# Fixed state places, a decay taken a step ahead and a pinned order in the state-space stage of a hybrid trunk layer

## The chip, the cores and the metric

The kernel runs on one core of a Trainium2 chip. The metric is the device time of one execution in microseconds, lower is better; the median of several runs is given. A core has five engines that run their own instruction queues in order and wait for each other through semaphores: TensorE (PE in the profile; its weight loads are listed apart as PEld), VectorE (DVE), ScalarE (ACT), GpSimd (POOL) and SyncE (SP), which here only issues DMA transfers. SBUF is the on-chip memory that all engines read; PSUM is the small memory of eight banks that TensorE writes its products to, and from which VectorE and ScalarE read.

## The reference

One layer of width 1024 on a sequence of 1024, everything in float32. A wide projection of the normalised input feeds two branches. The first (y_a) is a gated spatial mixer. The second (y_b) is a chunked state-space scan with 32 heads of 64 in 8 groups, a state of 128 and chunks of 128. Both are projected, gated, added and projected out. The part that matters here is the scan:

```python
decay = segsum_exp(adt)
cb = jnp.einsum('bclgn,bcsgn->bcgls', cc, bc)
y_diag = jnp.einsum('bcgls,bcgrls,bcsgrp->bclgrp', cb, decay, xd)
decay_to_end = jnp.exp(a_cs[..., -1:] - a_cs)
chunk_states = jnp.einsum('bcsgn,bcgrs,bcsgrp->bcgrpn', bc, decay_to_end, xd)
chunk_decay = jnp.exp(a_cs[..., -1])

def step(state, inp):
    cs, cd = inp
    return state * cd[..., None, None] + cs, state
...
y_off = jnp.einsum('bclgn,bcgrpn,bcgrl->bclgrp', cc, prev_states, jnp.exp(a_cs))
return (y_diag + y_off)
```

Then y_b gets the skip term (d_skip times x), is multiplied with silu(z) and RMS-normalised within its group.

## The kernel before

The kernel is one long program. Large products are made from three passes of a high and a low part of each operand ("hi" by ScalarE's copy, "lo" by VectorE's subtraction). It runs in stages: input and modulation, the wide projection (line 536), the state-space stage interleaved with the projection of y_a (this case), the projection of y_b (line 1548) and the output projection (line 1741).

**Order.** The instructions are written in Python and a planner decides the order on each engine from an estimated timeline. Two things bind it. `pin` (line 78) makes an instruction keep its program order among all pinned instructions of its engine: every TensorE instruction is pinned, and so are the loads on SyncE's queue. `tc.high_priority()` lets instructions go ahead of others that are ready. What is not pinned goes where the planner puts it. On the chip each queue is then strictly in order.

**The stage.** `order` (line 1202) lists 32 steps: two groups run interleaved, and each group has four steps of two chunks (256 positions). For step n the loop at line 1419 runs `front` of n, some units of the y_a projection (`draw`), `back` of n, `prep` of n + 2, the loads (`fetch`) of n + 5 and the decays of n + 3. A `draw` unit is two matmuls of `proj_a` (line 1355). Tasks given to `later(delay, ...)` run after so many slots; each `front`, `back` and `prep` is one slot.

- `fetch` loads the cumulative log decays (tile dcy, broadcast to all partitions) and the slab sl with six parts: C, B, two parts of x, two of silu(z). Five sets of these tiles rotate.
- `decay` (line 1058): ScalarE's exponential into ea (line 1063), GpSimd's triangular mask on dcy (line 1066), eight exponentials on dcy by ScalarE (line 1071).
- `prep` (line 1073): TensorE makes C·B and the transpose of B into bank pc and the transposes of x into bank px. VectorE makes xd and xe from px (line 1087) and multiplies dcy with C·B (line 1091); ScalarE copies the transposed B to tile bn (line 1093).
- `front` (line 1096): 16 matmuls give the within-chunk part in bank yi, then two or four give the chunk states in bank sp. For both chunks GpSimd multiplies the group's state with the chunk's decay into a new tile (line 1119) and VectorE adds sp to it (line 1121); the first state of a group is a copy (line 1117). The state tiles come from a rotation of four places over both groups (`st_r`).
- `back` (line 1125): eight matmuls (four in a group's first step) of the two states before the chunks with C give bank yn. `evacuate` (line 1138): VectorE adds the skip term to yi (y, line 1147) and multiplies yn with ea (ym, line 1151); GpSimd adds both (line 1152) and multiplies with silu(z) into yz (line 1153).
- `post` (line 1155): every second step of a group yz is stored; `squares` (line 1170) squares it in place on ScalarE (line 1172) and adds the halves on GpSimd (line 1173); `post2` sums over the group with TensorE and VectorE's ssq (line 1182).
- `proj_a` (line 1355): eight blocks of 8 x 3 units; at k = 1 of a block `wa_block` (line 1272) splits the weights of the next block: ScalarE's copy wah (line 1276) and VectorE's subtraction wal (line 1277), two of each. A block ends with the gate products tha on VectorE (line 1378).

Of the kernel before, what the change touches and what calls it, by code (L numbers as in the profile page):

```python
# [8 lines left out]
F32 = mybir.dt.float32  # L9
# [7 lines left out]
P = 128  # L17
# [18 lines left out]
def hybrid_kernel(  # L36
# [46 lines left out]
    def tp(dst, src, idn):  # L83
        pin(PE.transpose(dst, src, idn))  # L84
# [948 lines left out]
    NSET = 5  # L1033
    nstep, nst = [0], [0]

    class Group:
# [36 lines left out]
        def prep(self, s):  # L1073
            g, nm = self.g, f"{self.g}_{s}"
            sl, dcy, ea = self.pre[s]
            px, pc = bank(f"px{nm}"), bank(f"pc{nm}")
            for i in range(2):
                tsl = slice(i * P, (i + 1) * P)
                mm(pc[:, i * P : (i + 1) * P], sl[:, 1, tsl], sl[:, 0, tsl])
                tp(pc[:, 256 + i * P : 256 + (i + 1) * P], sl[:, 1, tsl], ident)  # L1080
                tp(px[:, i * 256 : i * 256 + P], sl[:, 2, tsl], ident)
                tp(px[:, i * 256 + P : i * 256 + 256], sl[:, 3, tsl], ident)
            x4 = px.rearrange("p (i h w) -> p i h w", i=2, h=HPG)
            xs = []
            for v, f in (("xd", dthq), ("xe", dde)):
                t = p2x.tile([P, 512], F32, name=f"{v}{nm}", tag=v, bufs=3)
                V.tensor_tensor(t.rearrange("p (i h w) -> p i h w", i=2, h=HPG), x4,
                                fac(f, g, s).unsqueeze(3).to_broadcast([P, 2, HPG, HD]), op=ALU.mult)
                xs.append(t)
            d3 = dcy.rearrange("p h i l -> p h (i l)")  # L1090
            V.tensor_tensor(d3, d3, pc[:, 0:256].unsqueeze(1).to_broadcast([P, HPG, 256]), op=ALU.mult)  # L1091
            bn = p2x.tile([P, 256], F32, name=f"bn{nm}", tag="bn", bufs=3)
            A.copy(bn, pc[:, 256:512])
            self.pre[s] = (sl, dcy, bn, xs[0], xs[1], ea)

        def front(self, s):
# [10 lines left out]
            sp = bank(f"sp{nm}")  # L1107
            self.y[s] = yi
            self.sts = [self.st]
            for i in range(2 if s < NCH // 2 - 1 else 1):  # L1110
                mm(sp[:, i * 256 : (i + 1) * 256], bn[:, i * P : (i + 1) * P], xe[:, i * 256 : (i + 1) * 256])
            for i in range(2 if s < NCH // 2 - 1 else 1):
                pool, tag, b = st_r[nst[0] % 4 if nst[0] % 4 < 3 else 2]
                nst[0] += 1
                s2 = pool.tile([P, 512 if pool is hp else 256], F32, name=f"st{nm}_{i}", tag=tag, bufs=b)[:, 0:256]
                if self.st is None:
                    V.tensor_copy(s2, sp[:, 0:256])
                else:
                    G.tensor_mul(v3(s2), v3(self.st),  # L1119
                                 fac(cd, g, s)[:, i].unsqueeze(2).to_broadcast([P, HPG, HD]))  # L1120
                    V.tensor_add(s2, s2, sp[:, i * 256 : (i + 1) * 256])  # L1121
                self.st = s2
                self.sts.append(s2)

        def back(self, s):
# [12 lines left out]
        def evacuate(self, s, yi, yn):  # L1138

# [4 lines left out]
            yz = self.yz[s // 2][:, :, (s % 2) * 256 : (s % 2 + 1) * 256]  # L1144
            y1 = turn(y1_r, f"y1{nm}", F32).rearrange("p (j t) -> p j t", j=2)
            for j in range(2):
                V.scalar_tensor_tensor(y1[:, j], sl[:, 2 + j], dskt[:, 2 * g + j : 2 * g + j + 1],
                                       yi[:, j * 256 : (j + 1) * 256], op0=ALU.mult, op1=ALU.add)
            m = turn(ym_r, f"ym{nm}", F32).rearrange("p (j t) -> p j t", j=2)
            t0 = 0 if s else P  # L1150
            V.tensor_tensor(m[:, :, t0:], yn.rearrange("p (j l) -> p j l", j=2)[:, :, t0:], ea[:, :, t0:], op=ALU.mult)  # L1151
            G.tensor_add(y1[:, :, t0:], y1[:, :, t0:], m[:, :, t0:])  # L1152
            G.tensor_mul(yz, y1, sl[:, 4:6])  # L1153

        def post(self, q):
# [105 lines left out]

    war_r, wah_r, wal_r = [], [], []

# [8 lines left out]
    def wa_block(dd):  # L1272
        was[dd] = []
        for i, wr in enumerate(war.pop(dd)):
            wh, wl = turn(wah_r[0], f"wah{dd}_{i}"), turn(wal_r[0], f"wal{dd}_{i}")
            A.copy(wh, wr)
            V.tensor_sub(wl, wr, f32(wh))
            was[dd].append((wh, wl))
# [76 lines left out]
    def proj_a():  # L1355

        for dd in range(KT):
# [8 lines left out]
            for k in range(KT):  # L1366
# [67 lines left out]

    room.extend(ea_r[0] + [st_r[0][1]])
    room.extend(tag for k in range(KT - 2) for tag in ya_tags[k])
# [441 lines left out]
```

## Time and profile before

| | |
|---|---|
| median of 3 runs | 1403.64 us (1401.98 to 1404.79) |
| the profiled execution, device time | 1405.65 us |
| its span in the profile | 1403.9 us |
| granted TensorE clock, mean | 0.995 |
| the state-space stage | 924 to about 1162 us of the span |

The page of the profile gives busy time and share per engine. A row of a group names line, engine, operation, output and input tiles with their shapes, the count, busy time and mean nanoseconds of one, and after a second bar the idle time before its instructions with what ended it. A row of waits names who waited for whom, microseconds in total, how often, and the longest. A row of a timeline gives the start, the duration, the instruction and in brackets its engine's idle time just before. A row of a stretch of time gives its length, then the busy time of PE, PEld, DVE, ACT and POOL with counts, then the granted clock, the DMA share and GB/s.

### The profile page before, as it was taken

How to read it: one execution, taken by the hardware profiler on the slowest of the kernel's cores; microseconds unless marked ns; L12 is line 12 of the kernel's file. 1: busy time of each engine (PE TensorE's matmuls, PEld its weight loads, DVE VectorE, ACT ScalarE, POOL GpSimd, SP SyncE). 2: the span in 40 equal slices, each digit the busy share in tenths (PEclk: the TensorE clock that was granted, in tenths of full speed). 3: DMA queues.
4: the chain of work that ended last, by engine and by line, in shares of the span. 5: the costliest groups of instructions: out<-in, count | busy, mean ns of one | idle time of the engine just before them, and what ended most of it. 6: DMA issues, size and time to landing. Idle time of an engine off the chain costs nothing.

```text
span 1403.9 us, 20510 instructions
## 1 busy us (share of the span) xinstructions
PE 1371.6 (98%) x6971; PEld 1134.5 (81%) x6971; DVE 1053.8 (75%) x1815; ACT 787.1 (56%) x1459; POOL 212.4 (15%) x208
## 2 busy tenths in 40 slices
PE   8999999999999999999999999999999999999997
PEld 7678888888888788787888888888888887888886
DVE  4777776687777889788888886388767765859976
ACT  5754656656656555455666555587766724223443
POOL 0000000000000011110100010027778750000001
PEclk9999999999999999999999999999999999999999
DMA  8675433343434777777665874498777758978913
GB/s 264 195 240 145 121 118 120 105 123 118 135 105 133 211 211 215 223 240 234 213 196 159 260 222 120 167 349 305 270 260 279 258 188 275 333 254 315 379 45 120
DMA packets 277182, 288.62 MB, mean 206 GB/s; under 512 B 15789, under 2 KB 224085, under 8 KB 277077
## 3 DMA queue, kind: packets, MB, share of 16 engines
q1 hardware_dynamic: 182420, 203.76, 45.8%
q10 hardware_dynamic: 94656, 83.54, 17.9%
q8 instruction: 55, 0.90, 0.3%
q14 instruction: 51, 0.41, 0.1%
HBM read 199.79 MB, written 87.46 MB: 205 GB/s over the span
## 4 chain that ended last, share of the span: by engine, by line
PE 67%; DMA 13%; DVE 9%; ACT 4%; issue 4%; POOL 2%; SPq 2%; ACTq 0%; DVEq 0%; POOLq 0%
PE xuz L536 6%; PE x L1548 6%; PE xcb L536 5%; PE yp L1548 5%; PE xx L536 4%; PE xz L536 4%; DMA wbr<-in_w_proj_b_dram 3%; PE vx L914 3%; PE xg L536 3%; PE yuz L536 3%; PE ycb L536 3%; PE pma L81 2%; PE ox L1741 2%; DMA dcy<-acs_d 2%; PE yx L536 2%
## 5 line engine op out<-in xcount | busy, mean ns | idle before, releaser
L755 POOL TENSOR_TENSOR wog<-wog,gb 128x256 f32<-128x256 f32 x16 | 16.7, 1062 | 625.1 <-DMA wog<-in_w_out_dram 625.1
L1071 ACT ACTIVATE dcy<-dcy,nacs 128x128 f32<-128x128 f32 x256 | 78.6, 389 | 14.7 <-POOL dcy L1066 14.2
L1066 POOL TENSOR_SCALAR_AFFINE_SELECT dcy<-dcy 128x1024 f32<-128x1024 f32 x32 | 35.0, 1093 | 136.8 <-ACT ea L1063 136.8
L986 ACT ACTIVATE ac<-ac 128x1024 f32<-128x1024 f32 x32 | 34.0, 1061 | 30.8 <-DVE ac L984 30.7
L1063 ACT ACTIVATE ea<-dcy 64x512 f32<-64x512 f32 x64 | 40.1, 626 | 13.0 <-DMA dcy<-acs_d 12.5
L81 PE MATMUL pma<-yh,wah 128*128 128x512 f32 x128 | 43.4, 420 | 0.0
L81 PE MATMUL pma<-yh,wal 128*128 128x512 f32 x128 | 42.6, 413 | 0.0
L1486 DVE SCALAR_TENSOR_TENSOR yn<-yn,par,rb 128x512 f32<-128x512 f32 x32 | 23.9, 748 | 24.6 <-DMA yn<-yb_d 24.6
L1091 DVE TENSOR_TENSOR dcy<-dcy,pc 128x1024 f32<-128x1024 f32 x32 | 38.9, 1217 | 4.4 <-PE pc L84 3.8
L1153 POOL TENSOR_TENSOR yz<-y,sl 128x512 f32<-128x512 f32 x32 | 41.4, 1293 | 1.1
L1151 DVE TENSOR_TENSOR ym<-yn,ea 128x512 f32<-128x512 f32 (+1 forms) x32 | 19.9, 623 | 28.5 <-PE yn L81 28.2
L81 PE MATMUL pma<-yl,wah 128*128 128x512 f32 x128 | 40.1, 394 | 0.0
L1152 POOL TENSOR_TENSOR y<-y,ym 128x512 f32<-128x512 f32 (+1 forms) x32 | 36.5, 1142 | 14.5 <-DVE ym L1151 13.7
L81 PEld LDWEIGHTS yn<-sl,st 128*128 128x128 f32 x224 | 30.2, 191 | 9.2 <-issue 2.9
L81 PE MATMUL yi<-dcy,xd 128*64 128x128 f32 x512 | 35.8, 283 | 1.8 <-DVE st L1121 1.8
L81 PE MATMUL yn<-sl,st 128*128 128x128 f32 x224 | 31.1, 276 | 6.0 <-DVE st L1121 6.0
L984 DVE SCALAR_TENSOR_TENSOR ac<-c2x,cwt,ac 128x1023 f32<-128x1023 f32 (+2 forms) x24 | 31.2, 1299 | 5.7 <-ACT ac L982 5.6
L81 PE MATMUL sp<-xe,bn 128*128 128x256 f32 x112 | 32.6, 408 | 2.7 <-DVE ssq L1182 1.5
L984 DVE SCALAR_TENSOR_TENSOR ac<-c2cb,cwt,ac 128x1023 f32<-128x1023 f32 (+2 forms) x24 | 31.1, 1294 | 4.4 <-ACT ac L982 4.3
L1119 POOL TENSOR_TENSOR st<-st,cd 128x256 f32<-128x256 f32 x48 | 32.9, 684 | 7.8 <-PE yn L81 5.5
L1756 POOL TENSOR_TENSOR r<-r,fnw 128x512 f32<-128x512 f32 x2 | 2.5, 1293 | 205.9 <-ACT junk L1754 205.9
L948 ACT ACTIVATE vm<-vm,vr 128x128 f32<-128x128 f32 x64 | 25.8, 484 | 14.0 <-DMA vm<-v_d 13.5
(2903 smaller groups left out, 4402.8 us busy)
## 6 DMA issues: line engine op xcount, KB each, us to landing
sl<-s_d SPq DMA_DIRECT2D x32, 768.0 KB
s_d<-ac ACTq DMA_DIRECT2D x32, 512.0 KB
dcy<-acs_d SPq DMA_DIRECT2D x32, 512.0 KB
av<-in_w_in_dram SPq DMA_DIRECT2D x36, 256.0 KB
aw<-in_ada_w_dram SPq DMA_DIRECT2D x16, 512.0 KB
wbr<-in_w_proj_b_dram SPq DMA_DIRECT2D x64, 128.0 KB
wb_d<-wbb ACTq DMA_DIRECT2D x32, 256.0 KB
wb_d<-wbc ACTq DMA_DIRECT2D x32, 256.0 KB
```

Of the source, the lines that this page charges most:

```text
L81: pin(PE.matmul(acc, l, r, start=first, stop=last))
L536: pin(PE.matmul(ps, lw[:, k * P : (k + 1) * P], r[k], start=first and n + k == 0, stop=n == 2 and k == 3, skip_group_check=not first))
L914: pin(PE.matmul(ps[pn][j], l[:, js], r, start=nm in ("p1", "p5", "p2") and n + k == 0, stop=n == 2 and k == 3, skip_group_check=nm not in ...
L984: V.scalar_tensor_tensor(ac[:, s:], cc[:, : S - s], conv_wt[:, 3 - s, i : i + 1], ac[:, s:], op0=ALU.mult, op1=ALU.add)
L986: A.activation(ac, ac, AF.Silu)
L1063: A.activation(ea[hh * HD : (hh + 1) * HD], dcy.rearrange("p (j e) i l -> p e j (i l)", e=2)[hh * HD : (hh + 1) * HD, hh], AF.Exp)
L1066: G.affine_select(out=d8, in_=d8, compare_op=ALU.is_ge, fill=-1e30, base=0, pattern=[[0, 2 * HPG], [1, P]], channel_multiplier=-1)
L1071: A.activation(dcy[:, h, i, :], dcy[:, h, i, :], AF.Exp, bias=sub[:, i, h : h + 1])
L1091: V.tensor_tensor(d3, d3, pc[:, 0:256].unsqueeze(1).to_broadcast([P, HPG, 256]), op=ALU.mult)
L1152: G.tensor_add(y1[:, :, t0:], y1[:, :, t0:], m[:, :, t0:])
L1153: G.tensor_mul(yz, y1, sl[:, 4:6])
L1548: pin(PE.matmul(ps[j], a[:, v, js], r, start=first and n + k == 0, stop=n == 2 and k == KT - 1, skip_group_check=not first))
```

## The change

The states of a group get three fixed places: one for the state in the middle of a step and two that alternate for the state at its end. The product of the end state with the next step's first decay is issued in `back`, into the middle place, right after yn has read it; `front` then adds sp into it in place. The y products move from `evacuate` to `front`, between the product and the sum of the end state. In `prep` the dcy product comes first, VectorE copies B behind it, and then come xd and xe; bn has two buffers in place of three. The instructions of `front`, `back`, `evacuate` and `prep` (but for the first step of the first two groups there) are pinned on VectorE and GpSimd. `squares` is due 8 slots after `post` in place of 5. The wal subtractions of blocks 1 to 7 are put in a list and issued, pinned, one at k = 3 and one at k = 4 of the block before.

```diff
@@ prep
+            keep = pin if s or g > 1 else lambda i: i
             x4 = px.rearrange("p (i h w) -> p i h w", i=2, h=HPG)
             xs = []
+            d3 = dcy.rearrange("p h i l -> p h (i l)")
+            keep(V.tensor_tensor(d3, d3, pc[:, 0:256].unsqueeze(1).to_broadcast([P, HPG, 256]), op=ALU.mult))
+            bn = p2x.tile([P, 256], F32, name=f"bn{nm}", tag="bn", bufs=2)
+            keep(V.tensor_copy(bn, pc[:, 256:512]))
             for v, f in (("xd", dthq), ("xe", dde)):
                 t = p2x.tile([P, 512], F32, name=f"{v}{nm}", tag=v, bufs=3)
-                V.tensor_tensor(t.rearrange("p (i h w) -> p i h w", i=2, h=HPG), x4,
-                                fac(f, g, s).unsqueeze(3).to_broadcast([P, 2, HPG, HD]), op=ALU.mult)
+                keep(V.tensor_tensor(t.rearrange("p (i h w) -> p i h w", i=2, h=HPG), x4,
+                                     fac(f, g, s).unsqueeze(3).to_broadcast([P, 2, HPG, HD]), op=ALU.mult))
                 xs.append(t)
-            d3 = dcy.rearrange("p h i l -> p h (i l)")
-            V.tensor_tensor(d3, d3, pc[:, 0:256].unsqueeze(1).to_broadcast([P, HPG, 256]), op=ALU.mult)
-            bn = p2x.tile([P, 256], F32, name=f"bn{nm}", tag="bn", bufs=3)
-            A.copy(bn, pc[:, 256:512])
@@ front
-            for i in range(2 if s < NCH // 2 - 1 else 1):
-                pool, tag, b = st_r[nst[0] % 4 if nst[0] % 4 < 3 else 2]
-                nst[0] += 1
-                s2 = pool.tile([P, 512 if pool is hp else 256], F32, name=f"st{nm}_{i}", tag=tag, bufs=b)[:, 0:256]
-                if self.st is None:
-                    V.tensor_copy(s2, sp[:, 0:256])
-                else:
-                    G.tensor_mul(v3(s2), v3(self.st),
-                                 fac(cd, g, s)[:, i].unsqueeze(2).to_broadcast([P, HPG, HD]))
-                    V.tensor_add(s2, s2, sp[:, i * 256 : (i + 1) * 256])
-                self.st = s2
-                self.sts.append(s2)
+            mid, *ends = state(g % 2)
+            if s == 0:
+                pin(V.tensor_copy(mid, sp[:, 0:256]))
+            else:
+                pin(V.tensor_add(mid, mid, sp[:, 0:256]))
+            self.sts = [self.st, mid]
+            self.st = ends[s % 2]
+            if not last:
+                pin(G.tensor_mul(v3(self.st), v3(mid), fac(cd, g, s)[:, 1].unsqueeze(2).to_broadcast([P, HPG, HD])))
+            self.y1 = y1 = turn(y1_r, f"y1{nm}", F32).rearrange("p (j t) -> p j t", j=2)
+            for j in range(2):
+                pin(V.scalar_tensor_tensor(y1[:, j], sl[:, 2 + j], dskt[:, 2 * g + j : 2 * g + j + 1],
+                                           yi[:, j * 256 : (j + 1) * 256], op0=ALU.mult, op1=ALU.add))
+            if not last:
+                pin(V.tensor_add(self.st, self.st, sp[:, 256:512]))
@@ back
-            self.evacuate(s, self.y.pop(s), yn)
+            if s < NCH // 2 - 1:
+                mid = state(self.g % 2)[0].rearrange("p (h w) -> p h w", h=HPG)
+                pin(G.tensor_mul(mid, self.st.rearrange("p (h w) -> p h w", h=HPG),
+                                 fac(cd, self.g, s + 1)[:, 0].unsqueeze(2).to_broadcast([P, HPG, HD])))
+            self.evacuate(s, self.y1, yn)
@@ evacuate
-            y1 = turn(y1_r, f"y1{nm}", F32).rearrange("p (j t) -> p j t", j=2)
-            for j in range(2):
-                V.scalar_tensor_tensor(y1[:, j], sl[:, 2 + j], dskt[:, 2 * g + j : 2 * g + j + 1],
-                                       yi[:, j * 256 : (j + 1) * 256], op0=ALU.mult, op1=ALU.add)
...
-            V.tensor_tensor(m[:, :, t0:], yn.rearrange("p (j l) -> p j l", j=2)[:, :, t0:], ea[:, :, t0:], op=ALU.mult)
-            G.tensor_add(y1[:, :, t0:], y1[:, :, t0:], m[:, :, t0:])
-            G.tensor_mul(yz, y1, sl[:, 4:6])
+            pin(V.tensor_tensor(m[:, :, t0:], yn.rearrange("p (j l) -> p j l", j=2)[:, :, t0:], ea[:, :, t0:], op=ALU.mult))
+            pin(G.tensor_add(y1[:, :, t0:], y1[:, :, t0:], m[:, :, t0:]))
+            pin(G.tensor_mul(yz, y1, sl[:, 4:6]))
@@ post
-                later(5, self.squares, yz, [yz[:, j] for j in range(2)])
+                later(8, self.squares, yz, [yz[:, j] for j in range(2)])
@@ wa_block
-            V.tensor_sub(wl, wr, f32(wh))
+            if dd == 0:
+                V.tensor_sub(wl, wr, f32(wh))
+            else:
+                lows.append((wl, wr, wh))
@@ proj_a
                 if k == 1 and dd + 1 < KT:
                     wa_block(dd + 1)
+                elif k in (3, 4) and lows:
+                    wl, wr, wh = lows.pop(0)
+                    pin(V.tensor_sub(wl, wr, f32(wh)))
@@ places of the states
-    st_r = [(hp, room.pop(0), 1), (p2x, "st", 1), (p2q, "st", 2)]
+    st_tag = room.pop(0)
+    st2 = hp.tile([P, 512], F32, name="st2", tag=st_tag)
+    sts = [st2[:, 0:256], st2[:, 256:512]]
+    sts += [pool.tile([P, 256], F32, name=f"st{n}", tag="st", bufs=2) for pool in (p2x, p2q) for n in range(2)]
+
+    def state(n):
+        return sts[n], sts[2 + n], sts[4 + n]
```

More of the change, by code (lines that the diff above doesn't have):

```diff
@@ L1033, in hybrid_kernel @@
     NSET = 5
-    nstep, nst = [0], [0]
+    nstep = [0]
     class Group:
@@ L1107, in front @@
             sp = bank(f"sp{nm}")
-            self.y[s] = yi
-            self.sts = [self.st]
-            for i in range(2 if s < NCH // 2 - 1 else 1):
+            last = s == NCH // 2 - 1
+            for i in range(1 if last else 2):
                 mm(sp[:, i * 256 : (i + 1) * 256], bn[:, i * P : (i + 1) * P], xe[:, i * 256 : (i + 1) * 256])
-            for i in range(2 if s < NCH // 2 - 1 else 1):
-                pool, tag, b = st_r[nst[0] % 4 if nst[0] % 4 < 3 else 2]
-                nst[0] += 1
-                s2 = pool.tile([P, 512 if pool is hp else 256], F32, name=f"st{nm}_{i}", tag=tag, bufs=b)[:, 0:256]
-                if self.st is None:
-                    V.tensor_copy(s2, sp[:, 0:256])
-                else:
-                    G.tensor_mul(v3(s2), v3(self.st),
-                                 fac(cd, g, s)[:, i].unsqueeze(2).to_broadcast([P, HPG, HD]))
-                    V.tensor_add(s2, s2, sp[:, i * 256 : (i + 1) * 256])
-                self.st = s2
-                self.sts.append(s2)
+            mid, *ends = state(g % 2)
[13 more added lines that the diff above has]
+                pin(V.tensor_add(self.st, self.st, sp[:, 256:512]))
         def back(self, s):
@@ L1260, in ya_operand @@
         yas.append((yh, yl))
-    war_r, wah_r, wal_r = [], [], []
+    war_r, wah_r, wal_r, lows = [], [], [], []
     def wa_load(dd):
```

4 lines of the change are left out of this document (2 added, 2 removed).

## The prediction

> **What bounds the kernel now.** I read the page first, then the busy times of the state-space stage (924 to 1162 us of the span), then who TensorE waited for there, then the timelines of the engines around those waits.
>
> ```profile
> span 1403.9 us, 20510 instructions
> PE 1371.6 (98%) x6971; PEld 1134.5 (81%) x6971; DVE 1053.8 (75%) x1815; ACT 787.1 (56%) x1459; POOL 212.4 (15%) x208
> ...
> 924.00:1162.00 238.00, 226.75 (x1661) 195.91 (x1659) 175.33 (x318) 152.88 (x391) 167.49 (x162) 0.99 0.78 270
> ...
> PE yn L81 <- DVE st L1121: 6.0, 4, 2.4
> PE yi L81 <- DVE st L1121: 1.8, 1, 1.8
> PE sp L81 <- DVE ssq L1182: 1.5, 1, 1.5
> PE sp L81 <- DVE xe L1087: 1.2, 2, 0.6
> PE pc L81 <- ACT bn L1093: 0.4, 1, 0.4
> ```
>
> TensorE is busy for 98% of the span and its program order is written by hand, so the time can only fall by what TensorE idles or runs slowly. In the stage that the change touches it is busy 226.75 of 238.00 us: 11.25 us of idleness, under 0.9% of the kernel. The change gives TensorE no less to do. So the question is which of the five waits above end, and what new ones come. Where they fall:
>
> ```profile
> 985.29 1.10 PE L81 MATMUL sp<-xe,bn 128*128 128x256 f32 x4 [0.63 <-DVE xe L1087]
> ...
> 1008.97 0.68 PE L81 MATMUL yn<-sl,st 128*128 128x128 f32 x4 [1.71 <-DVE st L1121]
> ...
> 1030.97 0.68 PE L81 MATMUL yn<-sl,st 128*128 128x128 f32 x4 [2.38 <-DVE st L1121]
> ...
> 1086.04 0.68 PE L81 MATMUL yn<-sl,st 128*128 128x128 f32 x4 [1.68 <-DVE st L1121]
> ...
> 1109.32 1.09 PE L81 MATMUL yi<-dcy,xd 128*64 128x128 f32 x16 [1.77 <-DVE st L1121]
> ```
>
> Each row is a start, a duration and, in brackets, the idle time before it. Three of the four yn waits make 1.71 + 2.38 + 1.68 = 5.77 us. On VectorE the same three places look alike:
>
> ```profile
> 1003.76 0.69 DVE L1277 TENSOR_TENSOR wal<-wa,wah 128x512 fp32r<-128x512 f32 x1 [2.23 <-ACT wah L1276]
> ...
> 1026.30 0.75 DVE L1277 TENSOR_TENSOR wal<-wa,wah 128x512 fp32r<-128x512 f32 x1 [2.04 <-ACT wah L1276]
> ...
> 1030.42 0.41 DVE L1121 TENSOR_TENSOR st<-st,sp 128x256 f32<-128x256 f32 x1
> ...
> 1081.36 0.76 DVE L1277 TENSOR_TENSOR wal<-wa,wah 128x512 fp32r<-128x512 f32 x1 [2.02 <-ACT wah L1276]
> ```
>
> VectorE stood for 2.0 to 2.2 us in front of the low part of a projection weight (wal), which needs ScalarE's copy wah; ScalarE was late. Behind it in VectorE's queue lay dcy, xd, xe, the two y products and only then the state sum st that TensorE's second half of yn needs: at 1030.42 for the wait that ends at 1030.97. So 5.77 us come from one cause, a subtraction that is not needed for several microseconds and blocks the queue. The yi wait has another chain:
>
> ```profile
> 1108.84 0.42 DVE L1121 TENSOR_TENSOR st<-st,sp 128x256 f32<-128x256 f32 x1 [4.66 <-POOL st L1119]
> ...
> 1107.14 1.09 POOL L1066 TENSOR_SCALAR_AFFINE_SELECT dcy<-dcy 128x1024 f32<-128x1024 f32 x1 [3.12 <-ACT ea L1063]
> ...
> 1105.28 0.63 ACT L1172 ACTIVATE yz<-yz 128x512 f32<-128x512 f32 x1 [2.69 <-DMA yb_d<-yz]
> ...
> ACT bn L1093 <- DVE dcy L1091: 22.6, 9, 6.3
> ACT yz L1172 <- DMA yb_d<-yz: 14.9, 10, 2.7
> ```
>
> ScalarE's square of yz is written over yz, so it waits (2.69 us) until the store of yz has read it; the exponential ea behind it is late, GpSimd's mask L1066 waits 3.12 us for ea, the state product behind the mask is late, and VectorE's sum waits 4.66 us. In all ScalarE loses 14.9 us of the stage to that store and 22.6 us to the copy of B (bn), which starts only when VectorE's dcy is done.
>
> **The change part by part.** The sum is made against the profiled execution, 1405.65 us (span 1403.9, so 1.75 lies around it). The median of the runs is 1403.64, 2.01 below it; I carry the difference over to the median.
>
> *Weight low parts.* The wal subtractions of all blocks but the first leave their place right behind ScalarE's copy (unit block k = 1 of the projection) and come one each at k = 3 and k = 4. Between k = 1 and k = 3 lie six projection units; a step draws four or five, so ScalarE gets over one step more, some 6 us or more by the yn starts 1008.97 and 1030.97 above (22.0 us, three steps apart, 7.3 us a step with its waits). It was late by 2.0 to 2.2 us. They are needed in the next block, some fourteen units later. Term: -5.8 us.
>
> *The clock.* The longest gap, 2.38 us, was followed by this:
>
> ```profile
> 1030.00:1032.00 2.00, 1.03 (x9) 1.04 (x10) 1.13 (x4) 1.99 (x7) 1.64 (x2) 0.96 0.54 117
> 1032.00:1034.00 2.00, 2.00 (x12) 1.67 (x13) 1.26 (x3) 0.42 (x1) 1.54 (x2) 0.50 1.00 403
> 1034.00:1036.00 2.00, 2.00 (x19) 1.72 (x16) 2.00 (x4) 1.41 (x5) 2.00 (x2) 0.68 0.37 145
> ```
>
> The column before the last two is the granted clock: 0.50 and 0.68 of full, so 2 x 0.50 + 2 x 0.32 = 1.6 us of TensorE's work were lost beside the gap. If the gap goes, this goes. Term: -1.6 us. The Trainium skill, "TensorE: Matmul & The Clock Gate", section "HAM oscillation — how this bites in real kernels", has as its abstract rule that idle gaps over about 3.4 us are what to avoid. By it a gap of 2.38 us would cost no clock, this term would be nought and the forecast 1.6 us later; the trace shows the half clock right behind the shorter gap, so the trace decides.
>
> *Squares three slots later (5 to 8).* A slot is one item of the step loop, three to a step, so a whole step more for the store. The longest wait is 2.69 us against a step of 6 to 7, so ScalarE's 14.9 us go. *B copied by VectorE, behind dcy.* ScalarE's 22.6 us go; VectorE gains 32 copies of 128x256 out of PSUM, whose price the same copy of a first state shows:
>
> ```profile
> L1117 DVE COPY st<-sp 128x256 f32<-128x256 f32 x8 | 3.3, 417 | 0.9 <-PE sp L81 0.9
> L1091 DVE TENSOR_TENSOR dcy<-dcy,pc 128x1024 f32<-128x1024 f32 x32 | 38.9, 1217 | 4.4 <-PE pc L84 3.8 <-issue 0.3
> L1121 DVE TENSOR_TENSOR st<-st,sp 128x256 f32<-128x256 f32 x48 | 19.8, 413 | 14.0 <-POOL st L1119 12.6 <-PE sp L81 1.4
> L1151 DVE TENSOR_TENSOR ym<-yn,ea 128x512 f32<-128x512 f32 x24 | 16.6, 690 | 26.0 <-PE yn L81 26.0
> ```
>
> 32 x 0.417 = 13.3 us. VectorE then works 175.3 + 13.3 = 188.7 us of a stage of some 228: 83%. The copy lies beside TensorE's work. Uncovered it would cost those 13.3 us; cover is the 26.0 us that VectorE now stands before ym until yn is done. B has two buffers in place of three: a new tile takes the place of one that sp read in the front just before on TensorE's own order, which costs nothing. Together these two end the yi wait (1.8) and the pc wait (0.4) that hung on a late ScalarE. Term: -2.2 us.
>
> *States in fixed places, decayed a step ahead.* As many GpSimd products and VectorE sums as before. The product for the first chunk of a step now runs right after the previous yn of its group, instead of at the new front. It waits for that yn to have read the place it writes; behind it on GpSimd lie the y sum and the yz product, but these need ym, which waits for the same yn, so the wait delays nobody. What stays on the path from sp to the second half of yn is one VectorE sum of 0.413 us; before, it had GpSimd's product ahead of it (12.6 us of waits in the 14.0 above). The y products move from the back to the front, where they need only yi, and cover the second GpSimd product: 2 x 0.472 us for the two halves against 0.684 us.
>
> ```profile
> L1119 POOL TENSOR_TENSOR st<-st,cd 128x256 f32<-128x256 f32 x48 | 32.9, 684 | 7.8 <-PE yn L81 5.5 <-DVE st L1117 2.1
> L1147 DVE SCALAR_TENSOR_TENSOR y<-sl,dskt,yi 128x256 f32<-128x256 f32 x64 | 27.6, 472 | 1.2 <-POOL yz L1153 1.2
> POOL dcy L1066 <- ACT ea L1063: 44.0, 20, 16.6
> ```
>
> yi's bank is also free sooner, which should end part of the sp waits (2.7 us in all): I take half, -1.35, between none and all.
>
> *Program order on both engines.* It adds waits that the planner's order avoided: dcy, bn, xd and xe now always stand behind ym, and ym behind the second state sum, which needs GpSimd. No row of before shows this order. Below, it costs nothing: TensorE needs a step's dcy, xd and xe only a whole step after their pc. Above, if each of 32 steps were 0.4 us longer, 12.8 us. I take 1.5 us, near the lower end, because at 83% VectorE has about 40 us of slack in 32 steps, over a microsecond in each, and every item has most of a step of lead.
>
> Sum: -5.8 - 1.6 - 2.2 - 1.35 + 1.5 = -9.4 us, so 1396.2 for the profiled execution and 1394.2 on the median. What is late next is sp behind xe and, at the end of the stage, the last gate product, neither of which is edited.
>
> **The rivals.** *(A) The fixed order eats half.* Each step loses 0.2 us to VectorE waiting in order (32 x 0.2 = 6.4 in place of 1.5): -4.5, 1399. For it: VectorE rises to 83% with no freedom to fill a wait. Against it: before, it waited 26.0 us for yn without harm.
>
> *(B) Nothing changes.* Masks, exponentials and squares stay with the planner, and the loads of the stage take a DMA share of 0.78 on average; and the chain of waits names the load of dcy with 2% of the span (row below); if the transfers set the pace, the waits come back elsewhere and the time stays within 0.2%, 2.8 us, which is about what a measurement of this kernel can tell from no change. Against it: not one of TensorE's five waits names a DMA. 1403.6.
>
> ```profile
> PE xuz L536 6%; PE x L1548 6%; PE xcb L536 5%; PE yp L1548 5%; PE xx L536 4%; PE xz L536 4%; DMA wbr<-in_w_proj_b_dram 3%; PE vx L914 3%; PE xg L536 3%; PE yuz L536 3%; PE ycb L536 3%; PE pma L81 2%; PE ox L1741 2%; DMA dcy<-acs_d 2%; PE yx L536 2%
> ```
>
> *(C) Slower: GpSimd's mask now stops VectorE as a whole.* GpSimd waited 44.0 us in 20 times for ScalarE's ea in front of a mask; without the longest, 27.4 us in 19, 1.44 each. A state product behind a waiting mask now holds the second state sum, and with it ym, dcy, bn, xd and xe in one row. If the fixed order leaves only 0.5 us of slack at those steps, 19 x 0.94 = 17.9 us reach TensorE in place of the 1.5, and the sum is +7.0: 1410.6. It decides from 1.08 us of mean wait (0.5 + 10.95 / 19) upwards. For it: the waits are above that now. Against it: of the nine waits of the state sum behind GpSimd, 12.6 us, just one reached TensorE, and the two things that made ScalarE late are taken away.
>
> **How the numbers follow.** Forecast 0.66, with a range of its own from 1390 (all 11.25 us of idleness and the clock's 1.6 gone, rounded) to 1397; A 0.16; B 0.06; C 0.12. Faster than 0.2% is forecast and A, 0.82; the same is B, 0.06; slower is C, 0.12. The range from 1390 to 1403 holds nearly all of the forecast, A and part of B, and leaves C out. The time is the forecast's, 1394.
>
> **What would show it.** TensorE's idle time in the stage falls from 11.25 us to about 3; no wait of VectorE for wah; no half clock between 924 and 1160; ScalarE's waits for the store of yz and for dcy gone; VectorE busy near 189 us in the stage. The prediction is wrong if TensorE waits for dcy, xd or st at many steps, by a few tenths each (A), or if GpSimd's waits for ea grow and VectorE's state sum waits behind them (C).

## The result and the profile after

The changed kernel takes 1409.15 us in the median of 7 runs (1401.63 to 1413.52), the kernel before 1403.62 (1400.51 to 1404.81) beside it. The ratio is 1.0046 [1.0027, 1.0065]: slower by about half a per cent. The prediction said 1394, in a range from 1390 to 1403. The profiled execution took 1409.15 us, with a span of 1407.4.

Where did the 3.5 us of span go? Three starts on TensorE cut each span: the first matmul of the y_a projection, the first of the y_b projection, and the first that takes a norm product of the second half (p3). First before, then after:

```profile
924.26 0.70 PE L81 MATMUL pma<-yh,wah 128*128 128x512 f32 x2
...
1160.21 0.39 PE L1548 MATMUL x<-p1bh,p1a 128*128 128x512 f32 x1
...
1187.52 0.39 PE L1548 MATMUL yp<-p3bh,p3a 128*128 128x512 f32 x1
```

```profile
921.24 0.70 PE L81 MATMUL pma<-yh,wah 128*128 128x512 f32 x2
...
1158.56 0.39 PE L1564 MATMUL x<-p1bh,p1a 128*128 128x512 f32 x1
...
1191.49 0.39 PE L1564 MATMUL yp<-p3bh,p3a 128*128 128x512 f32 x1
```

The stage took 235.95 us before (1160.21 - 924.26) and 237.32 after; the first eight units of the y_b projection (called the tail here) 27.31 and 32.93; the rest to the end 216.4 and 215.9. What came ahead of the stage was 3.0 us shorter in this execution, in code that the change does not touch (in the profiles of this document the stage starts anywhere from 919 to 925 us). So the stage, where 9 us were to be saved, lost 1.4, and 5.6 us were lost in a piece of program that nobody edited.

**The stage.** The busy times and TensorE's waits, to be set beside those of before:

```profile
924.00:1162.00 238.00, 227.25 (x1656) 196.70 (x1655) 183.67 (x346) 141.13 (x355) 167.00 (x162) 0.99 0.77 268
...
PE sp L81 <- DVE ssq L1185: 3.7, 3, 1.8
PE sp L81 <- DVE ym L1154: 2.8, 2, 1.4
PE yn L81 <- DVE st L1116: 2.3, 2, 2.1
PE yi L81 <- issue: 1.3, 2, 0.9
PE yn L81 <- DVE y L1123: 0.3, 1, 0.3
```

The waits named before add up to 10.9 us, these to 10.4. The yn waits fell from 6.0 to 2.6, as predicted in kind; but sp now waits 6.5 us for VectorE's ssq and ym, against 2.7. The waits of the other engines say why:

```profile
POOL dcy L1066 <- ACT ea L1063: 40.4, 18, 16.3
ACT ea L1063 <- DMA dcy<-acs_d: 31.2, 12, 7.2
DVE st L1126 <- POOL st L1120: 28.3, 17, 3.5
...
ACT yz L1175 <- DMA yb_d<-yz: 17.2, 13, 2.7
...
DVE ym L1154 <- PE yn L81: 7.5, 10, 1.6
...
DVE wal L1384 <- ACT wah L1279: 2.0, 1, 2.0
```

VectorE's wait for wah did go (8.2 us in 6 times before, 2.0 in one now). But its state sum now waits 28.3 us for GpSimd in place of 12.6, and its wait for yn, which was the slack that the prediction counted on, fell to 7.5 (28.2 over the same stretch before). One such place, GpSimd first, then VectorE and TensorE:

```profile
1011.30 1.64 POOL L1189 TENSOR_TENSOR ssq<-ssq,nhalf 128x8 f32<-128x8 f32 x1
1013.73 1.27 POOL L1176 TENSOR_TENSOR yz<-yz 128x512 f32<-128x512 f32 x1 [0.79 <-ACT yz L1175]
1014.95 0.61 POOL L1120 TENSOR_TENSOR st<-st,cd 128x256 f32<-128x256 f32 x1
```

```profile
1015.60 0.42 DVE L1126 TENSOR_TENSOR st<-st,sp 128x256 f32<-128x256 f32 x1 [3.27 <-POOL st L1120]
1015.94 0.68 DVE L1154 TENSOR_TENSOR ym<-yn,ea 128x512 f32<-128x512 f32 x1
...
1016.68 1.13 PE L81 MATMUL sp<-xe,bn 128*128 128x256 f32 x4 [1.39 <-DVE ym L1154]
```

The planner put the product of the end state behind a power and a sum of squares, which itself waited for ScalarE. VectorE, whose order is now fixed, stood 3.27 us in front of its second state sum, ym came late, and TensorE, which cannot write sp into the bank that ym still reads, waited 1.39 us.

**The tail.** VectorE and GpSimd in the changed kernel, then TensorE:

```profile
1170.84 0.75 DVE L1502 SCALAR_TENSOR_TENSOR yn<-yn,par,rb 128x512 f32<-128x512 f32 x1 [3.08 <-DMA yn<-yb_d]
...
1172.11 0.16 DVE L1185 TENSOR_SCALAR ssq<-yp 128x4 f32<-128x4 f32 x1
...
1178.20 0.75 DVE L1502 SCALAR_TENSOR_TENSOR yn<-yn,par,rb 128x512 f32<-128x512 f32 x1 [1.99 <-DMA yn<-yb_d]
1178.87 0.15 DVE L1185 TENSOR_SCALAR ssq<-yp 128x4 f32<-128x4 f32 x1
...
1179.10 1.65 POOL L1189 TENSOR_TENSOR ssq<-ssq,nhalf 128x8 f32<-128x8 f32 x1 [5.11 <-DVE ssq L1185]
...
1180.80 0.38 PE L84 MATMUL yp<-ident,ssq 128*8 128x128 f32 x1 [3.72 <-POOL ssq L1189]
```

TensorE had waited 0.76 us for the first of the two transposes already. The group sums of squares of the last two groups (ssq) go through GpSimd's power to a transpose on TensorE. The instruction order of VectorE shows that each ssq now stands behind one more norm product yn than before (nine and eleven in place of eight and ten), and that one waits for its load. In the kernel before the first of the two came 3.1 us earlier, though the stage had ended 1.7 us later, ahead of such a yn, and TensorE waited for neither:

```profile
1169.01 0.16 DVE L1182 TENSOR_SCALAR ssq<-yp 128x4 f32<-128x4 f32 x1
1172.81 0.75 DVE L1486 SCALAR_TENSOR_TENSOR yn<-yn,par,rb 128x512 f32<-128x512 f32 x1 [3.64 <-DMA yn<-yb_d]
```

None of these instructions is pinned, so their order is the planner's, and the planner moved them when the stage ahead of them changed. Behind the gap TensorE ran at half clock, as the windows of 2 us show (the column 0.50), which takes off another 2.6 us of its busy time (1.20 x 0.50 + 2.00 x 0.50 + 2.00 x 0.48):

```profile
1180.00:1182.00 2.00, 1.20 (x4) 1.01 (x5) 1.74 (x4) 0.62 (x1) 0.75 (x1) 0.50 0.12 37
1182.00:1184.00 2.00, 2.00 (x7) 1.52 (x6) 0.69 (x1) 0.00 (x0) 0.00 (x0) 0.50 0.01 2
1184.00:1186.00 2.00, 2.00 (x6) 1.60 (x5) 0.00 (x0) 0.00 (x0) 0.00 (x0) 0.52 0.19 59
```

### The profile page after: what moved, and what is told of

It is laid out like the page before. It is cut to its first block, busy times and chain, and to the rows that moved or that the text cites. A ratio compares the mean times of both kernels' runs of the same rounds, so it can differ in the third digit from the quotient of the medians.

```text
span 1407.4 us, 20533 instructions
## 1 busy us (share of the span) xinstructions
PE 1374.2 (98%) x6971; PEld 1137.8 (81%) x6971; DVE 1065.6 (76%) x1847; ACT 776.7 (55%) x1427; POOL 213.6 (15%) x208
## 4 chain that ended last, share of the span: by engine, by line
PE 69%; DMA 12%; DVE 8%; issue 3%; ACT 3%; POOL 3%; SPq 1%; ACTq 0%; DVEq 0%; POOLq 0%
PE xuz L536 6%; PE x L1564 5%; PE xx L536 5%; PE xcb L536 5%; PE yp L1564 5%; PE xz L536 4%; DMA dcy<-acs_d 3%; PE ox L1757 3%; PE vx L914 3%; PE xg L536 3%; PE yuz L536 3%; PE ycb L536 3%; PE yx L536 3%; PE oy L1757 2%; PE yz L536 2%
## 5 line engine op out<-in xcount | busy, mean ns | idle before, releaser
L755 POOL TENSOR_TENSOR wog<-wog,gb 128x256 f32<-128x256 f32 x16 | 17.7, 1120 | 621.2 <-DMA wog<-in_w_out_dram 600.5
L1063 ACT ACTIVATE ea<-dcy 64x512 f32<-64x512 f32 x64 | 40.1, 626 | 33.0 <-DMA dcy<-acs_d 31.2
L81 PE MATMUL pma<-yl,wah 128*128 128x512 f32 x128 | 40.4, 397 | 0.0
L984 DVE SCALAR_TENSOR_TENSOR ac<-c2x,cwt,ac 128x1023 f32<-128x1023 f32 (+2 forms) x24 | 31.2, 1299 | 5.7 <-ACT ac L982 5.5
L81 PEld LDWEIGHTS yi<-dcy,xd 128*64 128x64 f32 x512 | 28.0, 139 | 5.7 <-issue 4.3
L984 DVE SCALAR_TENSOR_TENSOR ac<-c1cb,cwt,ac 128x1023 f32<-128x1023 f32 (+2 forms) x24 | 31.1, 1295 | 1.3 <-ACT ac L982 1.3
```

The lines of the kernel that those rows point to most:

```text
L81: pin(PE.matmul(acc, l, r, start=first, stop=last))
L984: V.scalar_tensor_tensor(ac[:, s:], cc[:, : S - s], conv_wt[:, 3 - s, i : i + 1], ac[:, s:], op0=ALU.mult, op1=ALU.add)
L1063: A.activation(ea[hh * HD : (hh + 1) * HD], dcy.rearrange("p (j e) i l -> p e j (i l)", e=2)[hh * HD : (hh + 1) * HD, hh], AF.Exp)
```

## The experiments

Theory T: the tail's order, shifted by the planner, is what made the kernel slower. Theory S: the fixed order in the stage did, by rival C's mechanism. The other runs take the terms of the prediction's sum one by one. Each run was timed against the kernel before on the same chip, but not all on one chip, so two runs are best compared by their ratios; a profile is one execution, so where its stage and the median disagree, the median counts.

| run | edit | us, median | ratio to before |
|---|---|---|---|
| e1 | after, the two ssq of the tail ahead of yn | 1403.10 | 0.9986 [0.9968, 1.0003] |
| e2 | after, no pins in the stage | 1416.12 | 1.0091 [1.0066, 1.0116] |
| e3 | before, wal moved alone | 1405.45 | 1.0019 [1.0004, 1.0034] |
| e4 | after, B copied by ScalarE | 1408.60 | 1.0033 [1.0015, 1.0051] |
| e5 | e1, end product ahead of the squares | 1401.97 | 0.9988 [0.9977, 0.9998] |
| e6 | e5, masks and exponentials pinned too | 1428.36 | 1.0172 [1.0153, 1.0191] |
| e7 | e1, squares back at 5 slots | 1401.75 | 0.9990 [0.9978, 1.0001] |
| e8 | before, B copied by VectorE alone | 1409.00 | 1.0044 [1.0028, 1.0059] |
| e9 | e1, end product on VectorE | 1398.93 | 0.9959 [0.9945, 0.9973] |
| e10 | e9 and e5 together | 1401.70 | 0.9972 [0.9956, 0.9988] |
| e11 | e1, wal back in its place | 1404.98 | 1.0009 [0.9992, 1.0026] |
| e12 | e10, last gate product ahead of one yn | 1397.91 | 0.9964 [0.9950, 0.9979] |

### e1: the two ssq of the tail ahead of yn

```diff
-                V.tensor_scalar(ssq[:, g * NCH + q * 4 : g * NCH + q * 4 + 4], pq[:, 0:4], 1.0 / 256, EPS,
-                                op0=ALU.mult, op1=ALU.add)
+                (pin if len(sq) == 2 else lambda i: i)(
+                    V.tensor_scalar(ssq[:, g * NCH + q * 4 : g * NCH + q * 4 + 4], pq[:, 0:4], 1.0 / 256, EPS,
+                                    op0=ALU.mult, op1=ALU.add))
...
-        V.scalar_tensor_tensor(t, t, snw[:, n : n + 1], rbs[n // 2, h], op0=ALU.mult, op1=ALU.mult)
+        (pin if h == 1 and n >= 8 else lambda i: i)(
+            V.scalar_tensor_tensor(t, t, snw[:, n : n + 1], rbs[n // 2, h], op0=ALU.mult, op1=ALU.mult))
```

> The changed kernel, with VectorE's two late ssq instructions pinned ahead of the norms of the next product (p3), as they stood in the kernel before. Theory T (the loss sits behind the stage: TensorE waits 4.5 us for ssq in the projection of y_b because the planner put ssq behind norms that wait for loads, and the clock halves after it): those waits vanish, about 5.5 us go, 1403 to 1404 us, level with the kernel before. Theory S (the loss sits in the stage, in the fixed order): no more than 1 us goes, 1408 us.

The tail fell from 32.93 to 25.78 us with no wait of TensorE in it, the median from 1409.15 to 1403.10. The stage stayed as it was (237.6 us; VectorE's state sum waits 31.8 us for GpSimd); in it VectorE and GpSimd run the same order of instructions in both traces. T holds: the order in the tail alone turned a kernel that is level with the one before into a slower one. It is not quite the order of before: the second ssq stands behind eight yn here and behind ten there, and the tail of before (27.31 us) had a wait of 1.2 us for tha that is not in this one.

### e2: the planner's order in the stage

The edit takes every `pin` and `keep` of the change out of `prep`, `front`, `back` and `evacuate`.

> The changed kernel without the program order on VectorE and GpSimd in prep, front, back and evacuate; places, decay, copy of B, squares and weight low parts stay as changed. Theory S (the fixed order is what costs): VectorE's waits for GpSimd's state product fall from 28.3 us towards 13 us, the stage gets 5 us or more shorter, 1404 us or less. Theory T: the planner has ssq behind the norms here too, so the tail waits stay, 1407 to 1409 us.

Slower still, outside both ranges: 1416.12. The tail is the bad one (31.4 us), so the run compares with the changed kernel, 1409.15, and the pins are worth some 6 to 7 us. Without them the wait of VectorE's state sum for GpSimd falls to 19.2 us, but the stage takes 242.6 us and TensorE idles 14.3 us in it. S falls as a cause of the loss: the fixed order is the part that helps, given the rest.

### e3 and e11: the weight low parts

e3 is the kernel before with this step of the change alone; e11 is e1 without it:

```diff
-            if dd == 0:
-                V.tensor_sub(wl, wr, f32(wh))
-            else:
-                lows.append((wl, wr, wh))
+            V.tensor_sub(wl, wr, f32(wh))
```

> The kernel before, with only the weight low parts moved to k = 3 and k = 4. By the prediction's first two terms the three yn waits behind wal and the half clock after them go: 1396 to 1397 us. Rival: the wait for ScalarE only moves to the next instruction of VectorE that needs ScalarE or GpSimd, and TensorE's idleness in the stage stays near 11 us: 1402 to 1405 us.

> The kernel of e1 with the wal subtractions back behind ScalarE's copy, unpinned: all of the change but this step. Theory (under the fixed order the late place of wal saves what the prediction wanted, some 5 us, though alone on the kernel before it saved nothing in e3): VectorE stands for wah again, 6 us or more, and the time is 1405 to 1409. Rival (its place is worth nothing in either order): 1402 to 1404.5.

In e3 the waits for wah are gone and nothing is won: 1405.45. TensorE's waits:

```profile
PE yn L81 <- DVE st L1121: 6.4, 4, 1.8
PE pma L81 <- ACT bn L1093: 2.8, 1, 2.8
PE sp L81 <- DVE ssq L1182: 1.9, 1, 1.9
PE sp L81 <- DVE xe L1087: 1.6, 2, 1.0
```

The yn waits are 6.4 us as before (6.0), three of the four at other steps. (The profiled execution of e3 took 1409.76 us, longer than its median.) VectorE's waits for yn rose from 28.2 to 34.7 us and its state sum's waits for GpSimd from 12.6 to 14.5 when those for wah went. In e11, where the order is fixed, the old place gives a median about 2 us over e1 (1404.98 against 1403.10, from two chips, with intervals that overlap), and VectorE's waits change places again:

```profile
DVE st L1126 <- POOL st L1120: 14.7, 10, 3.7
DVE wal L1281 <- ACT wah L1280: 10.1, 6, 4.5
```

In e1 these are 31.8 and 2.0 us. So the step is worth nothing in the old order, and in the new one some 2 us by the medians, which the intervals do not tell from none.

### e4 and e8: who copies B

```diff
-            keep(V.tensor_copy(bn, pc[:, 256:512]))
+            A.copy(bn, pc[:, 256:512])
```

That is e4; e8 is the kernel before with `V.tensor_copy(bn, pc[:, 256:512])` in place of `A.copy`.

> The changed kernel with B copied by ScalarE again. The planner puts ssq where it stood in the kernel before. Theory T: 1403 to 1405 us, and no wait of TensorE for ssq behind the stage. Theory S with VectorE's load as the cause (13.3 us of copies): the stage gets several us shorter too, below 1402 us. If ScalarE's wait for dcy is what the copy's move was worth, the stage gets longer than the changed kernel's.

> The kernel before with the copy of B on VectorE and nothing else of the change (three buffers, not pinned). Theory (the copy is one of the change's good parts: with it ScalarE had a 5 us worse kernel in e4 than in e1): ScalarE's wait for VectorE's dcy ends, ea comes earlier, and the time is 1 to 4 us below the kernel before, 1400 to 1402.5. Rival (the gain appears only under the pinned order, where ScalarE's copy stood behind late squares; the planner's order hides it): 1403 to 1406, with 13 us more work on VectorE.

e4 has no wait for ssq in its tail (27.3 us): with an edit in `prep` alone its two ssq stand behind eight and ten yn again. It is 5.5 us above e1. But 4.4 us of its TensorE waits are one wait for the last gate product at the end of the stage, another accident of order, and the clock is at 0.50 and 0.73 in the 4 us behind it, some 1.5 us more (2 x 0.50 + 2 x 0.27). These two are as much as the whole difference, so what the copy itself is worth there is not shown. Alone, in e8, it makes the kernel before slower by 0.44%. VectorE's waits in e8:

```profile
DVE ym L1151 <- PE yn L81: 31.5, 23, 4.6
```

VectorE still waits 31.5 us for yn with 13 us more work. The work did not go into that slack: in the trace the copy lies between dcy and xd, in the row of instructions that ends in the state sum, and yn needs this sum. TensorE's yn waits were 9.5 us in six places.

### e5 and e6: GpSimd's order

e5 pins GpSimd's sum of the squares and its power and puts both behind a front, so that the end product has them behind it:

```diff
-                later(8, self.squares, yz, [yz[:, j] for j in range(2)])
-                later(17, self.post2, q, [yz[:, 0]])
+                later(9, self.squares, yz, [yz[:, j] for j in range(2)])
+                later(18, self.post2, q, [yz[:, 0]])
...
-            G.tensor_add(sq[0], sq[0], sq[1])
+            pin(G.tensor_add(sq[0], sq[0], sq[1]))
...
-                G.tensor_tensor(ssq[:, c8], ssq[:, c8], nhalf, op=ALU.pow)
+                (pin if g < NG - 2 else lambda i: i)(G.tensor_tensor(ssq[:, c8], ssq[:, c8], nhalf, op=ALU.pow))
```

> The kernel of e1 with GpSimd's sum of the squares and the power pinned, the squares due 9 slots after post in place of 8 and the group sum 18 in place of 17, so that both fall behind a front and GpSimd has the product of the end state (L1120) ahead of them. Theory (the fixed order makes VectorE's second state sum wait for a GpSimd that stands behind squares and powers): the wait of VectorE's st for POOL's st, 31.8 us in 18 times in e1, falls below 15 us, TensorE's sp waits for ym (3.1 us) go, the two half clocks behind them go, the stage falls from 237.6 us to 233 or less, and the time from 1403.1 to about 1398. Rival (the wait only changes places: ScalarE's ea and GpSimd's masks are as late as before, and what stands behind them is late): the st wait falls but TensorE idles as much, 9 us or more, and the time stays 1402 to 1404.

The stage fell to 234.5 us with no half clock, but the state sum's wait only from 31.8 to 27.1, TensorE idles 9.1 us, and the ratio did not move (0.9988 against 0.9986; the median is 1401.97): the rival was nearer. What stands ahead of the end product now, GpSimd and then VectorE in e5:

```profile
1059.34 1.09 POOL L1066 TENSOR_SCALAR_AFFINE_SELECT dcy<-dcy 128x1024 f32<-128x1024 f32 x1 [3.90 <-ACT ea L1063]
1060.39 0.61 POOL L1120 TENSOR_TENSOR st<-st,cd 128x256 f32<-128x256 f32 x1
...
1061.05 0.42 DVE L1126 TENSOR_TENSOR st<-st,sp 128x256 f32<-128x256 f32 x1 [4.92 <-POOL st L1120]
```

This is rival C to the letter: a mask that waits for ea, the product behind it, VectorE behind the product for 4.92 us. e6 then pins the masks, ea and the squares as well, with the decays issued behind the front:

```diff
             step(n, "front")
+            decays(n + 3)
...
-        decays(n + 4)
+        if n == 0:
+            decays(4)
```

> The kernel of e5 with ScalarE's squares and exponentials ea pinned too, and the decays of a later step (ea, mask) issued behind the front in place of the end of the step and the masks pinned there, so that no mask stands ahead of the end product. Theory (any GpSimd instruction that waits for ScalarE ahead of the end product holds VectorE): the st wait for POOL falls under 8 us and the time is 1 to 3 us below e5's. Rival (a fully pinned order loses more than it saves, because dcy then comes when it comes): ScalarE's exponentials and VectorE's dcy wait longer, TensorE waits for dcy or xd, and the time is above e5's by 2 us or more.

A clear miss, 1428.36, with a stage of 257.3 us. The state sum hardly waits (2.1 us), but the masks and with them the exponentials on dcy come too late:

```profile
ACT dcy L1073 <- POOL dcy L1068: 32.8, 23, 3.6
DVE dcy L1089 <- ACT dcy L1073: 28.6, 13, 4.2
PE yn L81 <- DVE st L1118: 15.2, 8, 4.6
```

In e5 the first of these is 20.3 us. Here a late mask costs far more than an early one in the wrong place.

### e7: the squares at 5 slots again

The edit is `later(5, self.squares, ...)` in e1.

> The kernel of e1 with the squares back at 5 slots. Theory (the three slots gave little: ScalarE's wait for the store of yz is 19.4 us with 8 slots in e1, 14.9 us with 5 in the kernel before, since the planner puts the squares where it likes): within 1.5 us of e1's 1403.1. Rival (the later squares did save their wait): ScalarE's wait for the store grows by 5 us or more over e1's and the time is 1405 or more.

1401.75 against 1403.10, ratios 0.9990 and 0.9986: the three slots do nothing. ScalarE waits 17.7 us for the store of yz with 5 slots and 19.4 with 8. The squares are not pinned; the delay moves where they stand in the program, not where the planner puts them: GpSimd runs the very same order in the stage of both.

### e9, e10 and e12: no GpSimd between the two sums

```diff
-                pin(G.tensor_mul(v3(self.st), v3(mid), fac(cd, g, s)[:, 1].unsqueeze(2).to_broadcast([P, HPG, HD])))
+                pin(V.tensor_mul(v3(self.st), v3(mid), fac(cd, g, s)[:, 1].unsqueeze(2).to_broadcast([P, HPG, HD])))
```

> The kernel of e1 with the product of the end state (L1120) on VectorE in place of GpSimd, in the same place of the pinned order; nothing else. VectorE then waits for no GpSimd instruction between the two state sums. Theory (what the fixed order costs is this one dependence, VectorE in order behind a GpSimd that stands behind masks, squares and powers): the 31.8 us of waits of e1 end, against 24 more products on VectorE of 0.4 to 0.7 us, 10 to 17 us, beside TensorE's work; TensorE's idle time in the stage falls from 10.6 us to 5 or less, no half clock, the stage 231 us or less, the time 1396 to 1399. Rival (the waits are slack: VectorE would have stood elsewhere, for yn or for the exponentials of dcy): VectorE's waits for yn and dcy grow by about what the others fall, TensorE idles 9 us or more and the time stays 1401 to 1404.

1398.93, ratio 0.9959 [0.9945, 0.9973]: faster than both kernels. The wait of 31.8 us is gone for 15.9 us of work:

```profile
L1120 DVE TENSOR_TENSOR st<-st,cd 128x256 f32<-128x256 f32 x24 | 15.9, 663 | 0.8
```

The median is in the theory's range, the profile's stage (234.8 us) is not: of its 9.7 us of idleness 5.3 are one wait of sp for an ssq, with a half clock behind it. (That execution, 1400.89 us, was the slowest of its eight.) e10 adds e5's places, which move those ssq:

> The kernel of e9 with e5's places of the squares and the group sums as well. Theory: the squares' place no longer matters for VectorE; what is left is the ssq behind which sp waits (2.9 to 3.7 us in all so far), which e5 turned into waits of pq for xe: within 1.5 us of e9. Rival (the places count by themselves): 2 us or more below e9.

Its stage took 231.4 us, but it won nothing over e9 (1401.70, above what either side expected). At the end of the stage VectorE had the last gate product tha behind a yn that waits for its load:

```profile
1160.59 0.50 PE L1566 MATMUL x<-p1bh,p1a 128*128 128x512 f32 x1 [2.73 <-DVE tha L1388]
```

and the clock fell behind it:

```profile
1162.00:1164.00 2.00, 2.00 (x6) 1.61 (x5) 2.00 (x4) 0.00 (x0) 0.00 (x0) 0.50 0.94 312
```

e12 pins that one yn, which puts it behind tha:

```diff
-        (pin if h == 1 and n >= 8 else lambda i: i)(
+        (pin if h == 1 and n >= 8 or (n, h) == (4, 0) else lambda i: i)(
```

> The kernel of e10 with one more norm product of y_b (yn of the fifth unit of the y_b projection) pinned, which puts it behind the last gate products tha on VectorE instead of ahead of them. In e10 the stage took 231.4 us, 3.4 less than in e9, but that norm stood 1.09 us for its load ahead of tha, TensorE waited 2.73 us for tha and then ran some 2 us at a lower clock, and the tail took 30.4 us in place of 25.8. Theory (the earlier end of the stage was lost to this one order): the wait is under 1.5 us with no low clock, the tail 26 to 28 us, the time 1396.5 to 1399.5. Rival (the y_b projection waits for its loads in any order, so an earlier end of the stage is worth nothing): TensorE waits as long for another operand of the tail and the time stays 1400.5 to 1402.5.

1397.91, ratio 0.9964 [0.9950, 0.9979], with the stage at 229.7 us and the tail at 27.3. TensorE's waits in the stage and the tail of e12:

```profile
PE pq L81 <- DVE xe L1092: 2.1, 3, 0.7
PE x L1566 <- DVE tha L1388: 1.3, 1, 1.3
PE yn L81 <- DVE y L1123: 1.1, 2, 0.7
PE px L84 <- DVE y L1123: 0.7, 1, 0.7
```

That is close to the stage the prediction had in mind: TensorE idles 4.3 us in it, at full clock. It took four edits more than the change has: the end product on VectorE, the squares and group sums behind the front, the ssq and one yn of the tail in place. VectorE is busy 200 of 230 us there. The differences in time between e9, e10 and e12 are within their intervals, so of these edits only the end product's is clear of noise, and that narrowly (e9 against e1).

## Why the prediction was wrong

Two steps failed. The largest term of the sum, the low parts with the half clock that hung on them (7.4 of 9.4 us), did not come: without the loss in the tail the change is worth about nothing (e1). And the program behind the edits, which the sum had at nothing, cost some 6 us. That the time came out near rival C's 1410.6 is luck and no proof of C: e1 keeps all the waits that C names and is level with the kernel before.

**The low parts (-5.8).** Right that VectorE's wait for wah would go, wrong that TensorE's wait goes with it. e3 shows the same 6 us of yn waits without any of it. The prediction read each yn wait back to one late instruction and took its wait off the sum; but the row that ends in the state sum has several waits, for yn, for GpSimd and for wah, and with one taken away the others grew (in e3, and between e11 and e1). In the fixed order the step brings some 2 us by the medians, not clear of noise (e11).

**The clock (-1.6).** The reading was right, the term fell with the one above. In the changed kernel a gap of 2.06 us is followed by this:

```profile
1028.00:1030.00 2.00, 1.77 (x11) 1.78 (x12) 2.00 (x4) 0.12 (x1) 1.85 (x2) 0.73 0.32 42
1030.00:1032.00 2.00, 2.00 (x16) 1.67 (x16) 2.00 (x4) 2.00 (x8) 0.93 (x1) 0.50 0.82 286
```

The half clock of the kernel before came back at about the same time, a second one at 1074 us followed a gap of 1.43 us, and the third is the tail's, behind 3.72 us. The rule of the Trainium skill that the prediction set aside ("TensorE: Matmul & The Clock Gate", section "HAM oscillation — how this bites in real kernels": gaps over about 3.4 us are what to avoid) differs here again: the clock fell behind gaps of 1.4 to 2.7 us. The length of a gap does not decide it alone, though: 2.46 us at 1061.52 in e5 and 2.84 us at 1108.74 in e8 were followed by the full clock. What else decides stays open, and so a half clock is no sure term of a sum.

**Squares and B (-2.2).** The squares do nothing (e7), because their place is the planner's. ScalarE's wait for dcy did end with the copy of B, but ea then waits for the load of dcy, 31.2 us in place of 12.5 (18.9 in e1). The statement that the copy is covered by the 26.0 us in which VectorE waits for yn was wrong in the old order: e8 prices it at +0.44% alone. That slack lies behind the copy in the same chain.

**States a step ahead (-1.35).** Not measured alone. The sp waits that were to halve went from 2.7 to 6.5 us; e5 and e9 change them by moving ssq and the end product. What the fixed places are worth by themselves stays open.

**Program order (+1.5).** The sign was wrong and the mechanism was right, in the wrong place. Given the other edits the order is worth some 6 to 7 us (e2). But part of rival C's mechanism is there: in the fixed order VectorE's state sum waits 27 to 35 us behind GpSimd (28.3 after, 31.8 in e1, 28.6 in e4, 27.1 in e5, 35.1 in e7), mostly behind squares, powers and masks; only where VectorE stands for wah (e11, 14.7) or the masks are pinned behind (e6, 2.1) is it less. Taking that one dependence away is worth some 4 us (e9 against e1). GpSimd's own wait for ea, from which C starts, did not grow (44.0 before, 40.4 after). The prediction had argued against C that the two things that made ScalarE late were taken away: the wait for the store stayed (17.2 us), and in place of the wait for dcy came a longer wait of ea for its load.

**What was not in the sum.** "What is late next is sp behind xe and, at the end of the stage, the last gate product, neither of which is edited" was the step that turned no gain into a loss: the prediction took what is not edited as unchanged. The tail is not edited, and it lost 5.6 us, because its order is made by a planner that sees the edited part before it. e1 shows what that order costs, by changing only it. Without it the median is within 0.2% of the kernel before, rival B's result (e1, 0.9986, with an interval that reaches from a small gain to none): what the parts of the change did to the stage together can hardly be told from nothing.

## What to carry to other kernels

Where a planner orders the instructions, an edit also moves what stands behind it: compare the order of every engine behind the edited part, and pin what a tightly timed stretch depends on. Every wait of an engine is a wait of all behind it in its queue, and in a fixed order the planner can no longer move work ahead of one, so take cross-engine dependences out of the fixed row first, even at the price of more work on that engine (24 products, 15.9 us of VectorE, for 31.8 us of waits). Idle time of an engine is cover for new work only if it lies beside the chain and not further down in it.

## What the runs showed of the hardware

The low part wal, whose two operands lie in SBUF, and GpSimd's instructions can hold each other up. VectorE and then GpSimd in the changed kernel:

```profile
1023.04 1.46 DVE L1384 TENSOR_TENSOR wal<-wa,wah 128x512 fp32r<-128x512 f32 x1
...
1022.86 1.09 POOL L1066 TENSOR_SCALAR_AFFINE_SELECT dcy<-dcy 128x1024 f32<-128x1024 f32 x1 [0.20 <-ACT ea L1063]
1023.92 1.74 POOL L1176 TENSOR_TENSOR yz<-yz 128x512 f32<-128x512 f32 x1
```

wal takes 0.68 us where GpSimd is still and 1.46 here: it starts beside the mask and ends 0.55 us after the mask's end (1023.95), and GpSimd's next instruction, which began in the meantime, takes 1.74 us in place of 1.27. The product ym, with an operand in PSUM, keeps its time beside GpSimd (at 1015.94 above 0.68 us, with GpSimd's product L1139 running from 1016.16; all 24 of this size took 0.67 to 0.69 us). The Trainium skill, "SBUF — State Buffer", section "🔬 SBUF: two separate sides", says that the port pair shared by the two engines is an exclusive lock, held for a whole instruction, against VectorE instructions with two operands in SBUF; these rows agree. It may be one reason why moving wal gave nothing in e3, where the sixteen took 16.2 us in place of 12.0, and why e9's products took 0.66 us on average and 0.42 at the shortest; neither was tested by itself.
